# Recurrence inputs and gates of a hybrid block: activations stationary, tokens on partitions, blocks of 512 columns turned by transposes

## Chip, cores and metric

The kernel runs on one core of one Trainium2 chip. The metric is the device time of one execution in microseconds (us), as the median of several runs. The engines are called PE (TensorE, the matmuls), DVE (VectorE), ACT (ScalarE) and SP (SyncE, which issues the DMAs here). GpSimd takes next to no part in this kernel.

## What is computed

One block of a network for 256 tokens of width 2048, in fp32: a normalisation with a modulation from a second input, a mixer with two branches (sparse attention with three key sets, and a gated linear recurrence), and a gated feed-forward part with a short convolution. The change touches the two projections that feed the recurrence, `lx` and `ly`:

```python
def rg_lru(x, w_a, b_a, w_i, b_i, lam):
    xb = x.reshape(bn, t, LRU_BLOCKS, LRU_BLOCK_DIM)
    r = sigmoid(einsum('btnd,nde->btne', xb, w_a).reshape(bn, t, w) + b_a)
    i = sigmoid(einsum('btnd,nde->btne', xb, w_i).reshape(bn, t, w) + b_i)
    log_a = (LRU_C * r) * log_sigmoid(lam)
    a = exp(log_a)
    b = sqrt(-expm1(2.0 * log_a)) * (i * x)
    ...                     # h[t] = a[t] * h[t-1] + b[t]
    return h

def token_mixer(h, w_in, ...):
    z = h @ w_in
    q, kc, vc, ks, vs, kw, vw, g_nsa, lx, ly, ga, gb = split(z, ...)
    o_a = nsa_attention(q, kc, vc, ks, vs, kw, vw, g_nsa, ...)
    u = causal_dwconv(lx, conv_w, conv_b)
    o_b = gelu(ly) * rg_lru(u, w_a, b_a, w_i, b_i, lam)
    merged = sigmoid(ga) * (o_a @ proj_a) + sigmoid(gb) * (o_b @ proj_b)
    return merged @ w_out
```

Both `lx` and `ly` are 256 tokens by 2048 features, each a product of the normalised input (256 by 2048) with 2048 columns of `w_in`.

## The kernel before

All weights stream from HBM once. `stage` (line 97) loads a piece of 128x2048 into one of four buffers `raw`, and `split` (line 102) makes two rounded parts of each half of it: `hi` on ACT and `lo`, the rest, on DVE (lines 107 and 108), three buffers of each. A dense product is then three matmuls per tile of weights, `hi` with the high part of the input, `hi` with its low part, and `lo` with its high part. The input `h1` has both parts side by side, 256 columns each, with features on partitions.

Two forms of dense product concern us. `dense_pair1` (line 171) holds the weights stationary, 128x128 at a time, and moves the 256 tokens through: the result has features on partitions and tokens in columns, which is what the convolution along time and the scan of the recurrence need. Two tiles of 128 features share one accumulator bank of 512 columns, so a call makes 256 features in one bank, with 96 matmuls of 256 columns (lines 184, 186, 187). `dense_tok` (line 191) holds the activations stationary, 128 tokens at a time, and moves 512 columns of weights: the result has tokens on partitions, 128 tokens by 512 features in each of two banks, with 96 matmuls of 512 columns (lines 202 to 204). The merge, the output projection and the down projection use it already; where they need features on partitions again, they turn 128x128 tiles with transposes on PE (lines 760 and 803).

The accumulators come from `bank` (line 111), four banks in rotation. The other four PSUM banks have tags: "s" (two banks), "t" and "o" (one each). Attention uses them for scores (s), transposed probabilities (t) and its output (o), and the recurrence for its gate matmuls (s, t and o).

The order of work around the change, as the program is written, is: four blocks of queries with one attention unit (`attention`, line 589, one of 8) behind each; then the first loop (line 668), eight calls of `dense_pair1` that make `lx`, copied to SBUF by ACT (line 670), each followed by an attention unit while there are any and by two fillers (`filler`, line 477: a piece of the modulation vector, one DMA and one DVE row product); then the second loop (line 679), four rounds of the recurrence on 512 features each. A round has the convolution on DVE (lines 694, 697), the gate matmuls (lines 699, 701), sigmoid, tanh, exp and sqrt on ACT (lines 705 to 711, each change of function kind loads a table), products and the scan on DVE (lines 712 to 716), then two calls of `dense_pair1` for `ly`, each followed by Gelu on ACT (line 721), the product with the scan on DVE (line 722), and a split of it into `oB` (lines 725, 726). Behind this the merge begins (line 735).

A planner reorders instructions of each engine ahead of time by priorities and a model of the chip; on the chip each engine takes its own row of instructions in that fixed order and waits for semaphores. Slots of SBUF are shared by tag: `lx` has the tags C4 to C7, and C7 is also the slot of `cmpb`, which holds the compressed keys and values (`kcmp`, `vcmp`) that each attention unit reads (lines 597, 647). The tiles `u`, `r`, `iu`, `tt` of the rounds have the slots of `qT`, `kT` and `vN` of attention.

## Time and profile before

| | us |
|---|---|
| median of 3 runs | 1811.32 (1810.37 to 1814.28) |
| profiled execution | 1810.84 |
| its span | 1809.0 |
| PE busy | 1788.1 |
| DVE busy | 1338.8 |
| ACT busy | 867.3 |

The span is the time from the first to the last instruction of the program in the profile; the device time has 1.8 us more around it. The busy time of an engine is the time in which at least one of its instructions ran. On PE, weight loads and matmuls overlap, and a matmul begins before the one ahead has left the array, so its duration in a row is longer than the step to the next start. A wait is the idle time of an engine ahead of an instruction, put down to what released it last. PE ran at a granted clock of 1.00 for all but the first microseconds.

### The profile page before, as it was taken

The page shows a single profiled execution, that of the slowest core. Times are in us where ns is not written, and L with a number is a line of the kernel's source. Part 1 is how long each engine was busy: PE and PEld are TensorE (multiplying, and loading weights), DVE is VectorE, ACT ScalarE, POOL GpSimd, SP SyncE. Part 2 cuts the span into 40 slices and gives each one's busy share as a digit, 9 for nine tenths or more (in the row PEclk, how much of TensorE's full clock was granted, in tenths as well). Part 3 has the DMA queues.
Part 4 walks back from the last instruction along what each step waited for, and adds up shares of the span by engine and source line. Part 5 has one row for each costly group of instructions (what it writes and reads, how often), then busy time and mean ns, then how long its engine had stood idle before and what let it go on. Part 6 is the DMA issues. An engine that isn't in the chain of part 4 may idle for free.

```text
span 1809.0 us, 25836 instructions
## 1 busy us (share of the span) xinstructions
PE 1788.1 (99%) x10344; PEld 1555.3 (86%) x10344; DVE 1338.8 (74%) x1942; ACT 867.3 (48%) x1176; POOL 0.2 (0%) x4
## 2 busy tenths in 40 slices
PE   8999999999999999999999999999999999999998
PEld 7899898788899888888888998888888888888886
DVE  7999866898788866767666898888555666666555
ACT  5645434655578443434445544444433444444443
POOL 0000000000000000000000000000000000000000
PEclk9999999999999999999999999999999999999999
DMA  9999862666556768787776566777655555555553
GB/s 357 366 333 361 316 245 96 214 227 210 210 175 222 273 241 292 282 285 284 294 278 209 172 231 235 277 279 279 249 190 189 188 189 189 191 190 190 186 189 113
DMA packets 64201, 429.51 MB, mean 237 GB/s; under 512 B 7089, under 2 KB 7377, under 8 KB 15569
## 3 DMA queue, kind: packets, MB, share of 16 engines
q1 hardware_dynamic: 63792, 427.08, 66.3%
q8 instruction: 81, 1.33, 0.3%
q10 hardware_dynamic: 288, 0.79, 0.1%
q14 instruction: 40, 0.32, 0.1%
HBM read 425.72 MB, written 2.11 MB: 237 GB/s over the span
## 4 chain that ended last, share of the span: by engine, by line
PE 94%; DVE 3%; DMA 1%; ACT 1%; issue 1%; DVEq 0%; ACTq 0%
PE P L130 17%; PE P L203 11%; PE P L204 11%; PE P L202 11%; PE P L131 9%; PE P L187 3%; PE P L184 3%; PE P L186 3%; PE P L426 2%; PE P L428 2%; PE P L427 2%; PE P L420 2%; PE P L421 2%; PE P L419 1%; PE P L148 1%; PE P L147 1%
## 5 line engine op out<-in xcount | busy, mean ns | idle before, releaser
L107 ACT ACTIVATE hi<-raw 128x1024 fp32r<-128x1024 f32 x589 | 623.2, 1060 | 808.9 <-PE P L204 322.0
L108 DVE TENSOR_TENSOR lo<-raw,hi 128x1024 fp32r<-128x1024 f32 x589 | 718.6, 1223 | 388.1 <-ACT hi L107 387.1
L130 PE MATMUL P<-h,hi 128*128 128x512 f32 x1344 | 465.9, 397 | 0.0
L131 PE MATMUL P<-h,lo 128*128 128x256 f32 x1344 | 362.8, 280 | 0.0
L130 PEld LDWEIGHTS P<-h,hi 128*128 128x128 f32 x1344 | 246.7, 188 | 53.2
L131 PEld LDWEIGHTS P<-h,lo 128*128 128x128 f32 x1344 | 253.6, 189 | 7.7
L233 DVE SCALAR_TENSOR_TENSOR raw<-raw,crow 128x2048 f32<-128x2048 f32 x64 | 146.3, 2286 | 13.0 <-DMA raw<-ada_w 13.0
L187 PE MATMUL P<-h,lo 128*128 128x256 f32 x512 | 147.1, 288 | 2.1 <-DVE lo L108 2.1
L184 PE MATMUL P<-h,hi 128*128 128x256 f32 x512 | 146.7, 287 | 0.0
L186 PE MATMUL P<-h,hi 128*128 128x256 f32 x512 | 146.6, 286 | 0.0
L426 PE MATMUL P<-h,hi 128*128 128x256 f32 x384 | 108.0, 286 | 0.0
L427 PE MATMUL P<-h,hi 128*128 128x256 f32 x384 | 107.3, 284 | 0.0
L428 PE MATMUL P<-h,lo 128*128 128x256 f32 x384 | 102.2, 284 | 0.0
L187 PEld LDWEIGHTS P<-h,lo 128*128 128x128 f32 x512 | 97.7, 191 | 3.9 <-DVE lo L108 2.6
L184 PEld LDWEIGHTS P<-h,hi 128*128 128x128 f32 x512 | 97.9, 191 | 3.3 <-issue 3.0
L186 PEld LDWEIGHTS P<-h,hi 128*128 128x128 f32 x512 | 97.9, 191 | 1.1 <-issue 1.0
L203 PE MATMUL P<-lo,ua 128*128 128x512 f32 x240 | 93.4, 389 | 0.0
L204 PE MATMUL P<-hi,ua 128*128 128x512 f32 x240 | 93.4, 389 | 0.0
L202 PE MATMUL P<-hi,ua 128*128 128x512 f32 x240 | 83.6, 389 | 0.0
L203 PE MATMUL P<-lo,h 128*128 128x512 f32 x192 | 75.5, 393 | 0.6 <-DVE lo L108 0.5
L204 PE MATMUL P<-hi,h 128*128 128x512 f32 x192 | 74.9, 390 | 0.0
L426 PEld LDWEIGHTS P<-h,hi 128*128 128x128 f32 x384 | 74.1, 193 | 0.2
(265 smaller groups left out, 3121.9 us busy)
## 6 DMA issues: line engine op xcount, KB each, us to landing
raw<-ada_w SPq DMA_DIRECT2D x96, 1024.0 KB, 5.0
raw<-w_up SPq DMA_DIRECT2D x96, 1024.0 KB, 4.9
raw<-w_down SPq DMA_DIRECT2D x48, 1024.0 KB, 4.9
raw<-w_lru SPq DMA_DIRECT2D x32, 1024.0 KB, 5.0
raw<-w_proj SPq DMA_DIRECT2D x32, 1024.0 KB, 5.0
raw<-w_gates SPq DMA_DIRECT2D x24, 1024.0 KB, 6.4
raw<-w_out SPq DMA_DIRECT2D x16, 1024.0 KB, 5.0
raw<-w_kv SPq DMA_DIRECT2D x24, 512.0 KB, 6.8
```

The costliest lines, as they stand in the source:

```text
L107: A.activation(hi[:, :n], raw[:, lo_col:lo_col + n], AF.Copy)
L108: V.tensor_tensor(lo[:, :n], raw[:, lo_col:lo_col + n], hi[:, :n].bitcast(F32), op=ALU.subtract)
L130: PE.matmul(ps[f], hi[:, sl], r, start=(kt == 0), stop=False, skip_group_check=True)
L131: PE.matmul(o, lo[:, sl], r[:, 0:256], start=False, stop=(kt == n - 1), skip_group_check=True)
L184: PE.matmul(o, hi[:, sl], r[:, 0:256], start=(kt == 0 and f == 0), stop=False, skip_group_check=True)
L186: PE.matmul(o, hi[:, sl], r[:, 256:512], start=False, stop=False, skip_group_check=True)
L187: PE.matmul(o, lo[:, sl], r[:, 0:256], start=False, stop=(kt == n - 1), skip_group_check=True)
L202: PE.matmul(ps[j], xh, hi[:, w], start=(kt == 0), stop=False, skip_group_check=True)
L203: PE.matmul(ps[j], xh, lo[:, w], start=False, stop=False, skip_group_check=True)
L204: PE.matmul(ps[j], xl, hi[:, w], start=False, stop=(kt == n - 1), skip_group_check=True)
L233: V.scalar_tensor_tensor(raw, raw, 1.0, row, op0=ALU.mult, op1=ALU.mult, accum_out=modc[:, c:c + 1])
L426: PE.matmul(o, hi[:, sl], h1[:, kt, 0:256], start=first and f % 2 == 0, stop=False, skip_group_check=True)
```

## The change

Both loops use `dense_tok` instead of `dense_pair1`, 512 features at a time, with the weights packed for it. A new helper, `turned`, makes eight transposes of 128x128 on PE that turn a block back, into two banks of the same rotation of four. In the first loop ACT copies the two banks of the product to SBUF (into the place where the turned block goes later), and then the two turned banks over them. In the second loop the Gelu takes the place of the first copy, and the DVE product reads the turned banks from PSUM. The first loop now has four rounds with two attention units and four fillers each; the fillers of the second loop stand behind a round. `dense_pair1` goes; `dense_pair` loses an option that nobody used.

```diff
+        def turned(rows):
+            ps = [bank("turn"), bank("turn")]
+            for f in range(4):
+                for j in range(2):
+                    o = (f % 2) * 256 + j * 128
+                    PE.transpose(ps[f // 2][:, o:o + 128], rows[:, j, f * 128:f * 128 + 128], ident)
+            return [p.rearrange("p (f t) -> p f t", f=2) for p in ps]
...
-        for pr in range(8):
-            pl = dense_pair1([w_lru[pr, k] for k in range(2)], h1r)
-            A.activation(lx[pr // 2][:, 2 * (pr % 2):2 * (pr % 2) + 2],
-                         pl.rearrange("p (f t) -> p f t", f=2), AF.Copy)
-            if units:
-                attention(*units.pop(0))
-            filler(2)
+        for bt in range(4):
+            ps = dense_tok([w_lru[bt, k] for k in range(4)], h1r)
+            rows = lx[bt].rearrange("p (j a) t -> p j (a t)", j=2)
+            for j in range(2):
+                A.activation(rows[:, j], ps[j], AF.Copy)
+            for h, p in enumerate(turned(rows)):
+                A.activation(lx[bt][:, 2 * h:2 * h + 2], p, AF.Copy)
+            for _ in range(2):
+                if units:
+                    attention(*units.pop(0))
+            filler(4)
...
-            for h in range(2):
+            ps = dense_tok([w_lru[4 + bt, k] for k in range(4)], h1r)
+            rows = u.rearrange("p (j a) t -> p j (a t)", j=2)
+            for j in range(2):
+                tbl(A.activation(rows[:, j], ps[j], AF.Gelu_apprx_tanh))
+            for h, p in enumerate(turned(rows)):
                 pr = bt * 2 + h
-                pl = dense_pair1([w_lru[8 + pr, k] for k in range(2)], h1r)
                 gl = u[:, 2 * h:2 * h + 2]
-                tbl(A.activation(gl, pl.rearrange("p (f t) -> p f t", f=2), AF.Gelu_apprx_tanh))
-                V.tensor_tensor(gl, gl, iu[:, 2 * h:2 * h + 2], op=ALU.mult)
+                V.tensor_tensor(gl, p, iu[:, 2 * h:2 * h + 2], op=ALU.mult)
...
-                filler(2 if pr % 4 == 0 else 0)
+            filler(2 if bt % 2 == 0 else 0)
...
-    a["w_lru"] = np.concatenate([_pack(w[:, 5168:7216]), _pack(w[:, 7216:9264])])
+    a["w_lru"] = _tok(w[:, 5168:9264])
```

The planner's order changes with it. Numbers behind a name tell buffers of one name apart; a row of the changed kernel has that kernel's own line numbers (L178 to L180 are the three matmuls of `dense_tok` there, L207 the transposes, L658 and L660 the copies of the first loop, L689 and L691 the gate matmuls, L710 the Gelu).

PE near the end of the first loop, before: the fourth head of the last attention unit but its tail (`tp`, transposed probabilities), its product with the compressed values (`oT_4438<-pcT_4461,cmpb_204`), and dense matmuls of the seventh and the eighth call (`P_4820`, `P_4946`).

```order
L643 MATMUL tp_4502<-cols_113,p_4491 128x128 x4
L647 MATMUL oT_4438<-pcT_4461,cmpb_204 128x512
L184 MATMUL P_4820<-h1_169,hi_4909 128x256
L186 MATMUL P_4820<-h1_169,hi_4909 128x256
L184 MATMUL P_4946<-h1_169,hi_4949 128x256
L186 MATMUL P_4946<-h1_169,hi_4949 128x256
L187 MATMUL P_4820<-h1_169,lo_4910 128x256
L184 MATMUL P_4820<-h1_169,hi_4909 128x256
```

The same place of the changed kernel, the last two attention units (`oT_4155`, `oT_4262`), the first gate matmuls of the recurrence (`lru_r`), and the first dense matmul of the second loop (`P_4793`) behind two transposes of the first loop's last block (`turn`).

```order
L629 MATMUL tp_4253<-cols_113,p_4242 128x128 x2
L689 MATMUL lru_r_4742<-lt_4736,raw_4740 128x256 x2
L637 MATMUL oT_4155<-pT_4180,vN_203 128x512 x2
L599 MATMUL tpc_4280<-cols_113,pc_4268 15x128 x4
L629 MATMUL tp_4304<-cols_113,p_4293 128x128 x4
L629 MATMUL tp_4326<-cols_113,p_4315 128x128 x4
L633 MATMUL oT_4262<-pcT_4285,cmpb_204 128x512
L689 MATMUL lru_r_4756<-lt_4736,raw_4740 128x256 x2
L207 MATMUL turn_4708<-cols_113,lx_3529 128x128
L207 MATMUL turn_4709<-cols_113,lx_3529 128x128
L178 MATMUL P_4793<-hi_4797,h1_169 128x512
```

Before, dense matmuls of two different banks stand around the last unit's product with `cmpb`. Now attention's rows follow each other from the first loop's last dense matmul to the transposes, and the second loop's first dense matmul stands behind these.

PE where one call for `ly` ends and the next one begins, before: the first two calls of the second loop (`P_5129`, `P_5259`).

```order
L184 MATMUL P_5129<-h1_169,hi_5218 128x256
L186 MATMUL P_5129<-h1_169,hi_5218 128x256
L187 MATMUL P_5129<-h1_169,lo_5219 128x256
L184 MATMUL P_5259<-h1_169,hi_5262 128x256
L186 MATMUL P_5259<-h1_169,hi_5262 128x256
```

The changed kernel: the end of the second loop's first block (`P_4794`, its second half of the tokens), gate matmuls of the next round, the first two transposes of the block (`turn`, from `lt_4736`, into which the Gelu writes), and the next block (`P_5014`).

```order
L179 MATMUL P_4794<-lo_4916,h1_169 128x512
L180 MATMUL P_4794<-hi_4915,h1_169 128x512
L689 MATMUL lru_r_4963<-lt_4959,raw_4961 128x256
L691 MATMUL lru_i_4964<-lt_4959,raw_4961 128x256
L689 MATMUL lru_r_4963<-lt_4959,raw_4961 128x256
L691 MATMUL lru_i_4964<-lt_4959,raw_4961 128x256
L689 MATMUL lru_r_4977<-lt_4959,raw_4961 128x256 x2
L691 MATMUL lru_i_4978<-lt_4959,raw_4961 128x256 x2
L207 MATMUL turn_4933<-cols_113,lt_4736 128x128
L207 MATMUL turn_4934<-cols_113,lt_4736 128x128
L178 MATMUL P_5014<-hi_5018,h1_169 128x512
```

Before, the next call follows in another bank with nothing between. Now the transposes of a block, which read what the Gelu wrote, stand ahead of the next block.

ACT ahead of the first Gelu of the second loop (L721 before), before: the chain of sigmoid, tanh, exp, sqrt with its table loads, and splits (L107) for later weights.

```order
L706 ACTIVATE lt_5074<-lru_i_5093,cols_113 128x256
L107 ACTIVATE hi_5218<-raw_5188 128x1024
L709 ACTIVATE lt_5075<-lt_5073 128x512
L107 ACTIVATE hi_5262<-raw_5260 128x1024
L710 ACT_TABLE_LOAD
L710 ACTIVATE lt_5073<-lt_5073 128x1024
L711 ACT_TABLE_LOAD
L711 ACTIVATE lt_5075<-lt_5075 128x1024
L107 ACTIVATE hi_5290<-raw_5260 128x1024
L107 ACTIVATE hi_5320<-raw_5318 128x1024
L721 ACT_TABLE_LOAD
L721 ACTIVATE lt_5072<-P_5129 128x512
```

The changed kernel, where the Gelu has L710 and reads the block `P_4793`, `P_4794`:

```order
L695 ACTIVATE lt_4737<-lru_r_4756,cols_113 128x256
L696 ACTIVATE lt_4738<-lru_i_4757,cols_113 128x256
L699 ACTIVATE lt_4739<-lt_4737 128x512
L700 ACT_TABLE_LOAD
L700 ACTIVATE lt_4737<-lt_4737 128x1024
L701 ACT_TABLE_LOAD
L701 ACTIVATE lt_4739<-lt_4739 128x1024
L107 ACTIVATE hi_5052<-raw_5050 128x1024
L710 ACT_TABLE_LOAD
L710 ACTIVATE lt_4736<-P_4793 128x512
L710 ACTIVATE lt_4736<-P_4794 128x512
```

The chain is the same; three of the splits that stood inside it are elsewhere now, and the last gate that it reads, `lru_i_4757`, comes from a matmul near the end of the same block.

## Rows read from the trace of the kernel before

**Rows 1.** The page: busy us (share) xinstructions; the last chain by engine.

```profile
PE 1788.1 (99%) x10344; PEld 1555.3 (86%) x10344; DVE 1338.8 (74%) x1942; ACT 867.3 (48%) x1176; POOL 0.2 (0%) x4
...
PE 94%; DVE 3%; DMA 1%; ACT 1%; issue 1%; DVEq 0%; ACTq 0%
```

**Rows 2.** Windows of the two loops: length, busy us (instructions) by engine, PE clock, DMA.

```profile
333.00:490.00 157.00, 157.00 (x1080) 130.63 (x1079) 130.07 (x336) 82.61 (x203) 0.00 (x0) 1.00 0.59 209
490.00:598.00 108.00, 105.94 (x831) 103.61 (x830) 92.35 (x131) 85.19 (x112) 0.00 (x0) 1.00 0.58 207
```

**Rows 3.** Waits of PE at 320 to 620 us: total, times, longest.

```profile
PE P L187 <- DVE lo L108: 2.1, 2, 1.5
```

**Rows 4.** Timeline of PE in the second loop, 256 columns: start, us, instruction.

```profile
559.92 0.28 PE L184 MATMUL P<-h,hi 128*128 128x256 f32 x1
...
561.96 0.28 PE L187 MATMUL P<-h,lo 128*128 128x256 f32 x1
```

**Rows 5.** Timeline of PE in the merge, dense_tok with 512 columns.

```profile
619.76 0.39 PE L202 MATMUL P<-hi,oB 128*128 128x512 f32 x1
...
625.88 0.39 PE L203 MATMUL P<-lo,oB 128*128 128x512 f32 x1
```

**Rows 6.** Timeline of PE: four transposes between dense matmuls of the merge.

```profile
921.46 0.39 PE L204 MATMUL P<-hi,mg 128*128 128x512 f32 x1
921.69 0.60 PE L760 MATMUL turn<-cols,sg 128*128 128x128 f32 x4
...
922.36 0.40 PE L204 MATMUL P<-hi,mg 128*128 128x512 f32 x1
```

**Rows 7.** Timeline of ACT: first chain of the second loop, with splits (L107).

```profile
494.66 0.46 ACT L706 ACTIVATE lt<-lru_i,cols 128x256 f32<-128x256 f32 x1
...
495.73 1.07 ACT L107 ACTIVATE hi<-raw 128x1024 fp32r<-128x1024 f32 x1
...
497.50 1.06 ACT L107 ACTIVATE hi<-raw 128x1024 fp32r<-128x1024 f32 x1 [0.18 <-ACT lt L709]
498.59 1.28 ACT L710 ACT_TABLE_LOAD   x1
...
504.50 1.06 ACT L107 ACTIVATE hi<-raw 128x1024 fp32r<-128x1024 f32 x1 [0.26 <-PE P L186]
...
506.88 0.60 ACT L721 ACTIVATE lt<-P 128x512 f32<-128x512 f32 x1
```

**Rows 8.** Timeline of PE: attention at 438 to 462 us; two rows a matmul.

```profile
441.77 1.02 PE L621 MATMUL s<-kT,qT 128*128 128x512 f32 x2
...
442.74 1.08 PE L621 MATMUL s<-kT,qT 128*128 128x512 f32 x2
...
445.69 1.12 PE L647 MATMUL oT<-pcT,cmpb 15*128 15x512 f32 x2
...
458.98 1.88 PE L651 MATMUL oT<-pT,vN 128*128 128x512 f32 x4
```

**Rows 9.** Chain of work in order of time: start, us, what (one gate matmul).

```profile
500.66 0.43 PE lru_r L699 x2
```

**Rows 10.** Timeline of ACT: attention at 438 to 462 us.

```profile
442.02 0.57 ACT L615 ACTIVATE pcT<-tpc 15x512 f32<-15x512 f32 x1
445.67 0.38 ACT L645 ACTIVATE pT<-tp 128x256 f32<-128x256 f32 x1 [3.08 <-PE tp L643]
446.90 0.48 ACT L633 ACTIVATE p<-s,sm 128x256 f32<-128x256 f32 x1 [0.85 <-DVE sm L631]
...
447.37 0.47 ACT L633 ACTIVATE p<-s,sm 128x256 f32<-128x256 f32 x1
```

**Rows 11.** Timeline of DVE, same stretch: a maximum over scores.

```profile
446.72 0.68 DVE L630 TENSOR_REDUCE sm<-s 128x2 f32<-128x512 f32 x1
```

**Rows 12.** Window near the start of the kernel.

```profile
19.80:23.00 3.20, 3.19 (x15) 3.20 (x16) 3.20 (x4) 0.90 (x1) 0.00 (x0) 0.51 0.96 373
```

**Rows 13.** Timeline of PE there; in brackets its wait and who ended it.

```profile
19.81 1.22 PE L426 MATMUL hold<-h,hi 128*128 128x256 f32 x4 [2.23 <-ACT h L291]
```

27 lines of the change are left out of this document (2 added, 25 removed).

## The prediction

> **What bounds the kernel now.** I read the page's shares first: TensorE (PE) is busy for 99% of the span, and the chain that ended last runs through it for 94% [rows 1]. So the time is what PE issues plus what it waits. The two loops that the change touches lie at 333 to 598 us [rows 2]. There PE is full, VectorE (DVE) has 83% and 86%, ScalarE (ACT) 53% and 79%. The view of waits shows 2.1 us of PE waiting in this stretch [rows 3]: work on the other engines costs nothing here until it makes PE wait. PE is pipelined, so the price of a matmul is not the duration in its row but the distance between two starts. The change leaves the bytes, the splits and the recurrence as they are, and the order of the instructions differs only between the last attention units and the end of the second loop.
>
> **Fewer, longer matmuls.** Before, a block of 512 features takes 4 x 16 x 3 = 192 matmuls of 256 columns. Seventeen steps from 559.92 to 561.96 are 2.04 us, 0.1200 us each [rows 4]. After, it takes 2 x 16 x 3 = 96 of 512 columns; twenty-seven steps from 619.76 to 625.88 are 6.12 us, 0.2267 us each [rows 5]. Two short ones cost 0.2400, one long one 0.2267: 13.3 ns go with each matmul saved. For 8 blocks that is 1536 x 0.1200 = 184.3 against 768 x 0.2267 = 174.1: **-10.2 us**, all of it on PE's path. Bounds: 0, if a long one takes as much as two short ones in these loops, and -10.2, the rows.
>
> A rule speaks against this size. The Trainium skill (TensorE: Matmul & The Clock Gate, section Back-to-back issue gap) gives a fixed cost of about 2.5 ns per matmul at the full clock; an estimate by that page is 768 x 2.5 ns = 1.9 us of gain instead of 10.2. The rows here show five times that, and I take the rows.
>
> **The transposes.** New on PE are 8 blocks x 8 = 64 transposes of 128x128. The kernel has the same instruction further down, four of them between two dense matmuls. From 921.46 to 922.36 pass 0.90 us where two dense steps would be 0.45, so four cost 0.45 and each further one 0.11 [rows 6]. The order puts them as 2 and 6 into each block: about 0.24 + 0.67 = 0.91, times 8 is **+7.3 us**. So the arithmetic alone gives -2.9 us, and waits of a few us decide the sign.
>
> **What ACT and DVE get.** The first loop gains 8 evictions of 128x512 on ACT, 0.60 us each [rows 7]: 4.8 us that lie in ACT's idle 74 us of that loop [rows 2]. In the second loop the Gelu count stays 8, and DVE's product reads PSUM instead of SBUF. These cost nothing as long as PE doesn't wait for them. It does once per block: the first two transposes stand right behind the block and need the eviction of its first half. Over these 0.60 us lie the six matmuls of the second half (1.36 us), unless ACT is inside a split of 1.06 us [rows 7]. Bounds: 0 and 8 x 1.06 = 8.5 us; I take a value near 0, since the cover is twice the eviction: **+0.9 us**.
>
> **Banks, the new wait.** Four accumulator banks rotate. Before, a block of 256 features takes one, so PE can be four blocks (46 us) ahead of ACT. After, a block of 512 takes two and its transposes two: the next block's accumulators are the two just filled, and PE can start on them only behind the evictions. Two evictions are late.
>
> *Place A, end of the first loop.* lx[3] has the slot of cmpb, which the last attention unit reads until its matmul with vcmp. Before, one bank waits for that and PE goes on in the next. After, both banks wait, and the order has a stretch of attention without a dense matmul ahead of the transposes. Its PE work from the first score matmul: four scores at 0.97, two value products at 0.86, two with pcT at 1.05 [rows 8], four gate matmuls at 0.43 [rows 9] and 20 transposes at 0.11 [rows 6], together 11.7 us. The chain through the softmax is longer. In it two exps take 1.0 us, a copy of a turned tile 0.3, oA and pcT some 0.55 each [rows 10], a maximum 0.6 to 0.7 [rows 11], a table load 1.28 [rows 7]. Walking down PE's, ACT's and DVE's rows with these, from that score matmul: the exps of head 0 end at 3.7, of head 1 at 5.0 (the third and fourth scores wait for their bank), of head 2 at 7.2 (the gate matmul waits for its bank), table and sigmoid at 9.2, oA and pcT (behind the value products) at 11.0, the next copies at 12.4, table and exps of head 3 at 14.7, two copies at 15.3, the block's eviction at 15.8. PE's transposes come at 15.9, not 11.7: **+4.3 us** of waits in some eight pieces. Bounds: 0 if other work covers them, 7 if DVE's conv rows, which stand among the softmax rows, hold it up.
>
> *Place B, end of the second loop's first block.* As attention ends inside this block, the recurrence's first chain starts late in it. The last three sigmoids follow a gate matmul that has only 10 dense (2.3 us) and 8 gate matmuls (3.4 us, [rows 9]) behind it; then come the transposes, which need the Gelu. Before, from the first of the three sigmoids at 494.66 to the Gelu's end at 507.48 passed 12.8 us, with three splits of together 3.1 in them that now stand elsewhere [rows 7]: 9.7, and some 0.4 from PE to ACT and back. The Gelu ends 10.1 us behind that matmul, against 5.7 of work: **+4.4 us** in one piece, bounds 0 and 6. Before, it came with PE already in the next bank. In the later blocks the chain starts at the block's beginning and lies under 22.7 us of PE work.
>
> **The sum.** The profiled execution took 1810.84 us (span 1809.0 and 1.8 around it), 0.5 under the median 1811.32. 1810.8 - 10.2 + 7.3 + 0.9 + 4.3 + 4.4 = **1817.5 us**. The 2.1 us of old waits are left in: they came from splits late on DVE, whose load stays. 0.2% of the time before is 3.6 us (about what a measurement can tell from no change), so "same" is 1807.7 to 1814.9.
>
> **Rivals.**
> 1. *Only one of the two waits is there.* If attention ends earlier against the dense work than I read from the order, B goes, or A's pieces are covered: 1817.5 - 4.4 = 1813.1, no change. For it: both are sums of short pieces, and PE may come to these rows late enough that the softmax is done. Against: A's waits follow from PSUM tags one deep inside the stretch, whoever comes first.
> 2. *Faster: the banks don't bind.* Every eviction comes in time, because ACT and DVE stay ahead of PE as they are now; it decides from waits under about 1 us in all. Then -2.9 + 0.9, and the old 2.1 us gone as well: 1806 to 1809, middle 1807. For it: ACT has nearly half its time free in the first loop [rows 2]. Against: ACT takes its rows in order, and the order itself has the stretch without dense work.
> 3. *The clock falls.* After a wait of 2.23 us that ended at 19.8 us, PE ran at a granted clock of 0.51 (1.2 of 2.4 GHz) for 3.2 us [rows 12, 13], which loses half of these, 1.6 us. If B, or B and A, sets that off: 1819.1 to 1820.7. The same page of the Trainium skill (section Why this matters for your kernels) warns of idle gaps between bursts of matmuls for this reason; the rows at 19.8 us agree.
> 4. *The cost per matmul is not saved.* If a long matmul took as much as two short ones here, the first term is 0: 1810.8 + 7.3 + 0.9 + 8.7 = 1827.7. The spacings speak against it [rows 4, 5]. By the 2.5 ns of the page above it would be 1825.8.
>
> That the change doesn't do what it says is out: the order shows the 768 and the 64 instructions.
>
> **Chances.** Forecast 0.50; one wait only 0.25; faster 0.13; clock 0.07; no saving per matmul 0.05. Slower by over 0.2% is 0.50 + 0.07 + 0.05 = 0.62, within it 0.25, faster 0.13. The forecast's own range is 1814.9 to 1822. For 8 in 10 the range goes down into the faster case and up past the clock case and A's upper bound: 1807 to 1824. Left out are the lower half of the faster case, the case without saving and the tail.
>
> **What the profile after would show.** Dense starts 0.227 us apart and transposes 0.11: the terms -10.2 and +7.3. PE's waits in this stretch: a sum near 9 to 12 us, the longest one ahead of the first transposes of the second loop, released by the Gelu (B), and several under 1 us among the last attention rows, released by exps, copies and the first loop's last eviction (A). Behind the second loop nothing differs. I am wrong in B if the Gelu of that block ends before PE's last gate matmul, in A if PE has no gap over 0.2 us among the last attention rows, and in the arithmetic if the spacings differ.

## The result

The changed kernel takes 1828.66 us (median of 4 runs, 1826.01 to 1829.28), the kernel before 1811.60 in the same comparison: a ratio of 1.0087, 95% interval 1.0075 to 1.0100. It is slower, as forecast, but by 17 us and not by 6.7, and the time lies above the range. The profiled execution took 1829.13 us with a span of 1827.3.

The page of the changed kernel, busy times and the last chain (to compare with [rows 1]):

```profile
PE 1797.0 (98%) x9640; PEld 1524.0 (83%) x9640; DVE 1341.7 (73%) x1942; ACT 878.4 (48%) x1188; POOL 0.2 (0%) x4
...
PE 92%; DVE 3%; ACT 2%; DMA 1%; issue 1%; DVEq 0%; ACTq 0%
```

PE has 704 instructions less (1536 dense ones before; 768 dense ones and 64 transposes after), and yet is busy for 9 us more. Part of the reason is the clock: at half clock the same instruction keeps PE busy longer. Windows of the changed kernel between 477 and 551 us (length, busy us and instructions of PE, weight loads, DVE, ACT and POOL, then the granted clock, the DMA share, GB/s):

```profile
477.00:490.00 13.00, 10.60 (x40) 5.79 (x39) 11.15 (x38) 9.31 (x23) 0.00 (x0) 0.85 0.00 1
486.00:492.90 6.90, 6.90 (x16) 4.29 (x16) 2.43 (x11) 2.97 (x9) 0.00 (x0) 0.51 0.00 0
527.00:530.40 3.40, 2.99 (x8) 2.47 (x9) 1.38 (x2) 3.37 (x7) 0.00 (x0) 0.50 0.01 2
547.50:550.90 3.40, 3.40 (x10) 2.66 (x9) 3.40 (x6) 1.06 (x1) 0.00 (x0) 0.50 0.69 280
```

The last three run at half clock (1.2 of 2.4 GHz); in both loops of the kernel before it was 1.00 [rows 2]. The first is place A: forty matmuls in 13 us, hardly a transfer. The view of waits for PE at 333 to 614 us, the two loops of the changed kernel (to compare with [rows 3]: what waited, for what, total, times, longest):

```profile
PE P L179 <- DVE lo L108: 5.1, 5, 1.9
PE turn L207 <- ACT lt L710: 3.9, 1, 3.9
PE lru_r L689 <- ACT p L619: 0.9, 1, 0.9
PE tp L629 <- ACT pT L631: 0.7, 1, 0.7
PE tp L629 <- ACT pcT L601: 0.7, 1, 0.7
PE P L178 <- ACT hi L107: 0.2, 1, 0.2
```

The second row is place B, in one piece, released by the Gelu (L710). The next three are place A. The first row was not in the forecast: late splits, 2.1 us before, are 5.1 now.

**Where 18 us went.** I took every step from one start on PE to the next, between the transposes of the gate tile (`gtp`, at 288 us, ahead of both loops) and those of `mq` (in the merge, 647 us before, 664 after). A step's usual length for its kind is *work*; in a stretch at half clock, up to the same length again is *clock*; the rest is *waits*. This is arithmetic on the trace's rows, the same for each kernel; which length is taken as usual moves up to about 1 us from one column to another, mostly between clock and waits, and leaves the sum as it is. The stretch is 17.9 us longer: work -3.2, clock +6.2, waits +14.9. Of the waits 10.6 us lie in steps stretched by over 0.25 us (A 2.9, B 4.0, and late splits some 4 more than before); the other 4.3 us are many short ones, which the view of waits doesn't name. Behind the stretch another 0.4 us come.

**The path.** The attention's last product starts 195.2 us behind the gate tile in the kernel before, 221.9 us in the changed one; from there to the first matmul of the merge's projections it is 114.2 us before, 104.2 now. So attention ends 26.6 us later; about 10 us of this are made good in the second loop, and 16.7 reach the projections. Why it ends later is seen in the turns of one attention unit's four heads. Timeline of PE, the transposes `tp`, before:

```profile
445.26 0.38 PE L643 MATMUL tp<-cols,p 128*128 128x128 f32 x2
...
449.00 0.38 PE L643 MATMUL tp<-cols,p 128*128 128x128 f32 x2
...
452.50 0.38 PE L643 MATMUL tp<-cols,p 128*128 128x128 f32 x2
...
455.89 0.38 PE L643 MATMUL tp<-cols,p 128*128 128x128 f32 x2
```

The same in the changed kernel:

```profile
448.53 0.60 PE L629 MATMUL tp<-cols,p 128*128 128x128 f32 x4
...
454.34 0.60 PE L629 MATMUL tp<-cols,p 128*128 128x128 f32 x4
...
459.94 0.60 PE L629 MATMUL tp<-cols,p 128*128 128x128 f32 x4
...
464.65 0.60 PE L629 MATMUL tp<-cols,p 128*128 128x128 f32 x4
```

A head takes 3.5 us before and 5.4 us now. Between two such steps the instruction order has some 20 dense matmuls in both kernels: 2.4 us of 256 columns, 4.5 us of 512. The planner has put as many between as before, each nearly twice as long. So the order differs from the first loop's start on, and not only from the last attention units on.

### The profile page after: what moved, and what is told of

It reads as the page before. It is cut to its first block, busy times and chain, and to the rows that moved or that the text cites. A ratio compares the mean times of both kernels' runs of the same rounds, so it can differ in the third digit from the quotient of the medians.

```text
span 1827.3 us, 24410 instructions
## 1 busy us (share of the span) xinstructions
PE 1797.0 (98%) x9640; PEld 1524.0 (83%) x9640; DVE 1341.7 (73%) x1942; ACT 878.4 (48%) x1188; POOL 0.2 (0%) x4
## 4 chain that ended last, share of the span: by engine, by line
PE 92%; DVE 3%; ACT 2%; DMA 1%; issue 1%; DVEq 0%; ACTq 0%
PE P L126 17%; PE P L179 14%; PE P L180 14%; PE P L178 14%; PE P L127 9%; PE P L412 2%; PE P L413 2%; PE P L414 2%; PE P L406 2%; PE P L407 2%; PE P L405 1%; PE P L144 1%; PE P L143 1%; PE P L145 1%; PE oT L637 1%; PE s L607 1%
## 5 line engine op out<-in xcount | busy, mean ns | idle before, releaser
L107 ACT ACTIVATE hi<-raw 128x1024 fp32r<-128x1024 f32 x589 | 622.6, 1060 | 814.3 <-PE P L180 360.0
L127 PE MATMUL P<-h,lo 128*128 128x256 f32 x1344 | 362.8, 280 | 0.0
L126 PEld LDWEIGHTS P<-h,hi 128*128 128x128 f32 x1344 | 246.8, 188 | 53.2
L127 PEld LDWEIGHTS P<-h,lo 128*128 128x128 f32 x1344 | 253.6, 189 | 7.7
L179 PE MATMUL P<-lo,h 128*128 128x512 f32 x448 | 180.1, 402 | 5.7 <-DVE lo L108 5.7
L180 PE MATMUL P<-hi,h 128*128 128x512 f32 x448 | 177.5, 396 | 0.0
L178 PE MATMUL P<-hi,h 128*128 128x512 f32 x448 | 166.9, 400 | 0.6 <-ACT hi L107 0.6
L219 DVE SCALAR_TENSOR_TENSOR raw<-raw,crow 128x2048 f32<-128x2048 f32 x64 | 146.3, 2286 | 11.3 <-DMA raw<-ada_w 11.2
L412 PE MATMUL P<-h,hi 128*128 128x256 f32 x384 | 108.2, 286 | 0.0
L179 PEld LDWEIGHTS P<-lo,h 128*128 128x128 f32 x448 | 85.2, 190 | 27.2 <-DVE lo L108 9.3
L413 PE MATMUL P<-h,hi 128*128 128x256 f32 x384 | 107.6, 284 | 0.0
L414 PE MATMUL P<-h,lo 128*128 128x256 f32 x384 | 102.1, 284 | 0.0
L178 PEld LDWEIGHTS P<-hi,h 128*128 128x128 f32 x448 | 85.1, 191 | 18.7 <-ACT hi L107 1.6
L180 PEld LDWEIGHTS P<-hi,h 128*128 128x128 f32 x448 | 85.1, 190 | 18.4 <-issue 1.5
L180 PE MATMUL P<-hi,ua 128*128 128x512 f32 x240 | 93.4, 389 | 0.0
L178 PE MATMUL P<-hi,ua 128*128 128x512 f32 x240 | 83.6, 389 | 0.0
L412 PEld LDWEIGHTS P<-h,hi 128*128 128x128 f32 x384 | 74.1, 193 | 0.2
L413 PEld LDWEIGHTS P<-h,hi 128*128 128x128 f32 x384 | 74.2, 193 | 0.0
L308 DVE SCALAR_TENSOR_TENSOR raw<-raw,crow 128x2048 f32<-128x2048 f32 x31 | 70.8, 2285 | 2.4 <-DMA raw<-ada_w 2.1
```

Source lines behind the costliest of these rows:

```text
L107: A.activation(hi[:, :n], raw[:, lo_col:lo_col + n], AF.Copy)
L126: PE.matmul(ps[f], hi[:, sl], r, start=(kt == 0), stop=False, skip_group_check=True)
L127: PE.matmul(o, lo[:, sl], r[:, 0:256], start=False, stop=(kt == n - 1), skip_group_check=True)
L178: PE.matmul(ps[j], xh, hi[:, w], start=(kt == 0), stop=False, skip_group_check=True)
L179: PE.matmul(ps[j], xh, lo[:, w], start=False, stop=False, skip_group_check=True)
L180: PE.matmul(ps[j], xl, hi[:, w], start=False, stop=(kt == n - 1), skip_group_check=True)
```

## Experiments

All times are compared with runs of the kernel before on the same chip (median 1810.9 to 1812.0 in the five comparisons). The table has the ratio with its interval (from all runs), and from the one profiled execution the sums as defined above (against before, us) and the path: the start of the attention's last product behind the gate tile, and from there to the first projection matmul.

| kernel | ratio (95%) | work | clock | waits | attention ends | then |
|---|---|---|---|---|---|---|
| before | 1 | 0 | 0 | 0 | 195.2 | 114.2 |
| after | 1.0087 (1.0075–1.0100) | -3.2 | 6.2 | 14.9 | 221.9 | 104.2 |
| e1 first loop only | 1.0113 (1.0095–1.0131) | -1.7 | 8.7 | 13.9 | 223.5 | 104.2 |
| e2 second loop only | 1.0034 (1.0021–1.0047) | -1.7 | 0 | 7.9 | 195.9 | 118.0 |
| e3 slot freed | 1.0110 (1.0095–1.0126) | -3.2 | 6.7 | 17.5 | 229.5 | 99.7 |
| e4 copy first | 1.0071 (1.0057–1.0085) | -3.2 | 0 | 16.0 | 219.4 | 98.7 |
| e5 halves | 1.0090 (1.0076–1.0104) | 6.9 | 0 | 8.0 | 196.1 | 127.0 |
| e6 paced | 1.0070 (1.0058–1.0083) | -3.2 | 4.6 | 12.3 | 214.5 | 107.3 |
| e7 filled wait | 1.0134 (1.0118–1.0149) | 0.9 | 7.1 | 15.9 | 221.9 | 109.2 |
| e9 before, no tables | 0.9990 (0.9980–1.0000) | -0.2 | 0 | -1.7 | 195.4 | 112.2 |
| e10 second loop, no tables | 1.0035 (1.0022–1.0047) | -1.7 | 1.6 | 5.1 | 195.2 | 118.0 |
| e11 after, no tables | 1.0037 (1.0023–1.0050) | -3.2 | 0 | 8.8 | 219.0 | 94.7 |
| e12 second loop, not turned | 1.0028 (1.0016–1.0040) | -5.1 | 3.1 | 7.8 | 195.7 | 119.4 |
| e13 second loop, turned pairs | 1.0140 (1.0126–1.0154) | 3.3 | 4.1 | 17.0 | 195.3 | 138.5 |
| e17 second loop, spread | 1.0037 (1.0024–1.0050) | -1.7 | 0 | 9.5 | 195.2 | 118.3 |
| e18 spread, copy first | 1.0051 (1.0039–1.0064) | -1.7 | 3.2 | 8.8 | 195.8 | 121.4 |

The profiled execution also differs by up to 3.4 us ahead of the gate tile, where no kernel was changed; the sums and the path leave this out, the ratios do not.

### One loop at a time

e1 has `dense_tok` and `turned` in the first loop alone, e2 in the second alone.

> The first loop as after, the second loop as before. Theory (place A costs waits and also a clock drop, and both belong to the first loop): half of the arithmetic, about -1 us, place A's waits +4, one stretch of 6.8 us at 1.2 GHz +3.3, and no wait for a Gelu ahead of transposes: about +6, 1818 us (1816 to 1820), granted clock 0.5 once, near the end of the attention. Rival 1 (nearly all of the loss is made in the second loop): 1811 to 1813 us. Rival 2 (attention that ends late harms the second loop whatever its form): 1821 us or more, with several us of waits behind the attention.

> The second loop as after, the first loop as before. Theory (the second loop has its own wait at its first block, the recurrence's chain being longer than the PE work behind the gate matmuls): -1 us of arithmetic, 2 to 3 us of wait ahead of the first transposes, later split waits of some 2 to 3 us more than before, one clock drop of 1.7 us at most: 1815 us (1813 to 1818). Rival 1 (the second loop only inherits the late attention of the first): no wait over 1 us there, no drop of the clock, 1809 to 1811 us. Rival 2 (the second loop makes nearly all of the loss by itself): 1822 us or more.

The first loop alone costs as much as the whole change, if not more: 1832.55 us (the intervals meet). It has attention 28 us late. At the end of attention, at 480 to 504 us, lie 17.0 of its 20.4 us at half clock, and then a second loop of the old form pays as well, with a wait of 5.0 us for a late split:

```profile
PE P L180 <- ACT hi L107: 5.3, 2, 5.0
```

That is rival 2 of e1, and my theory fell. The second loop alone took 1817.72 us, some 6 us over before (ratio 1.0034), with the clock at 1.00 in both loops; its waits at 333 to 640 us:

```profile
PE P L199 <- DVE lo L108: 4.9, 6, 1.6
PE turn L227 <- ACT lt L726: 0.9, 3, 0.3
```

So place B needs the late attention (three waits of at most 0.3 us here), and the second loop has a loss of its own, most of it late splits (4.9 of 7.9 us of waits). The time of e2 lies in my range, but not for my reason: the wait of 2 to 3 us ahead of the first transposes, on which the range was built, isn't there.

### Place A: the slot, or the order

e3 moves `kcmp` and `vcmp` out of C7. e5 cuts each dense matmul of the loops in two and leaves all else. e6 frees the slot, keeps 512 columns, writes all attention units ahead of the first loop and ties that loop's dense matmuls behind the attention's steps.

```diff
-        kcmp = cmpb[:, 256:316]
-        vcmp = cmpb[0:16, 316:828]
+        kcmp = small["gap5"][:, 0:60]
...
+            c3.append(big.tile([128, 1024], F32, tag="C3", name="c3"))   # e3: vcmp in its upper half
```

```diff
+                    for c in range(cut):                                  # e5: cut=2 in the two loops
+                        z = 512 // cut
+                        w, o = slice(k * 512 + c * z, k * 512 + c * z + z), ps[j][:, c * z:c * z + z]
```

```diff
+                    if pace and k == 0:                                   # e6, order only
+                        i = calls[0] * 36 // 64 - 3
...
+                            tc.add_manual_dep(m.ins, marks[i].ins.name, NOSYNC, reason="pace")
```

> The kernel after, with the compressed keys and values moved out of slot C7 (keys into a spare column range, values into the unused half of slot C3), so that lx[3] has its slot to itself. Theory (place A is the shared slot with both banks blocked): the stretch of attention without dense work goes from the end of the first loop, with it its waits of about 4 us and the stretch at 1.2 GHz behind them (3.3 us); the wait ahead of the first transposes of the second loop stays or grows by 1 to 2 us: about 1822 us (1820 to 1824). Rival 1 (the clock falls for another reason than the waits): the drop near 486 us stays and the time is 1825 us or more. Rival 2 (the attention's own chain sets the end, and the wait only moves behind the next block): 1827 to 1830 us, no change.

> The kernel after, but each dense matmul of the two loops cut into two of 256 columns; layout, transposes and bank use as after. The instruction order of this kernel has the attention steps between the dense matmuls as the kernel before has them (some 20 dense matmuls between two steps, which take 2.4 us here and 4.5 us with 512 columns), and no stretch of attention without dense work. Theory (what is lost is the order: as many dense matmuls stand between two steps of the attention as before, each twice as long, so attention ends some 27 us late and is left bare): dense work back to its 184 us, 64 transposes at +7 us, the waits of place A and the clock drops gone: about 1818 us (1816 to 1821), faster than after although TensorE has 10 us more of dense work. Rival 1 (banks and transposes make the waits): all waits and drops stay and the dense work adds its 10 us: 1837 us. Rival 2 (only place A belongs to the order, the second loop's waits belong to the banks): 1824 us.

> The kernel after with 512 columns kept, the slot C7 freed for lx[3], and the dense matmuls of the first loop tied in groups of six to the steps of the attention units by order alone (no semaphore), so that about half as many stand between two steps. Theory (the order makes the loss): attention ends near 490 us instead of 509 us, no bare stretch at its end, no clock drop in the loops beyond one at most; what is left is the second loop's waits as in the kernel with the second loop alone: 1811 to 1816 us. Rival 1 (512 columns, banks and turning cost it whatever the order): 1824 us or more. Rival 2 (the second loop's waits follow from the late attention too): 1809 us or less.

e3 took 1831.73 us. The stretch of bare attention went from the first loop's end, but came back behind the next block: at 509 to 514 us three steps of 0.89 to 1.32 us stand among attention's rows (the third row below has two of them), with 6.8 us at half clock from 512 us on, and a longer wait came at place B. Its view of waits, 333 to 640 us:

```profile
PE turn L207 <- ACT lt L711: 6.0, 2, 5.6
PE P L179 <- DVE lo L108: 3.9, 4, 1.8
PE tp L630 <- ACT pT L632: 1.8, 2, 1.1
```

Attention ended even later (229.5), so the slot and the banks only decided where TensorE waits for it: rival 2, whose range (1827 to 1830) the time lies a little above.

e5 has the same layout, transposes and banks as after and 10 us more work, and is not slower than after (1827.30). Attention ends at 196.1 us again, the place A waits are gone, and the clock stays at 1.00 in the loops. Its heads, timeline of PE:

```profile
449.83 0.38 PE L632 MATMUL tp<-cols,p 128*128 128x128 f32 x2
...
453.28 0.38 PE L632 MATMUL tp<-cols,p 128*128 128x128 f32 x2
...
456.78 0.38 PE L632 MATMUL tp<-cols,p 128*128 128x128 f32 x2
```

3.5 us a head, as before: the length of the matmuls between the steps, whose number stays, makes attention late, not layout, banks or slot. But the time is 9 us above my 1818, and above rival 2's 1824: 8.0 us of waits stay, 4.6 of them late splits in the view of waits. So the second loop's waits don't go with attention's late end, as e2 (waits 7.9) says too. e6 points the same way with 512 columns: fewer matmuls between the steps bring attention's end back by 7.4 us against after, and by 15.0 against e3, which frees the slot too. Its time of 1824.51 is not what I hoped for (1811 to 1816) and lies where rival 1 has it: a bare stretch of attention moved to the start of the loop (350 us, 3.4 us at half clock), and a wait of 3.6 us for `hi` came in the second loop, with 6.8 us at half clock behind it. It brought back 7.4 of 26.6 us only, so it doesn't decide between theory and rival 1; e5 does, for attention.

### Place B: the Gelu on TensorE's path

e4 copies a block out of its banks at once, turns it, and takes the Gelu of the turned block; this adds two copies of 128x512 per round on ACT. e7 puts 18 matmuls ahead of the first transposes of the second loop, in the place of the wait.

```diff
+            with tc.high_priority(200):                                   # e4
+                for j in range(2):
+                    A.activation(rows[j], ps[j], AF.Copy)
...
+                tbl(A.activation(gl, p, AF.Gelu_apprx_tanh))
```

```diff
+            for n in range(extra):                                        # e7: extra=18 in the first round
+                m = PE.matmul(ps[0], h1r(n % KT)[:, 0:128], h1r(n % KT), start=True, stop=True, skip_group_check=True)
+                tc.add_manual_dep(m.ins, behind.ins.name, NOSYNC, reason="behind the gates")
```

> The kernel after, with the second loop's blocks copied out of their banks at once (a Copy ahead of the queued rows, into two spare tiles), turned, and the Gelu taken of the turned block. Theory (place B is the transposes waiting for a Gelu at the end of the recurrence's chain): the wait of 3.9 us ahead of the first transposes goes, and the clock drop behind it (1.7 us); the later split waits of 6 to 7 us, which follow from the chain being bunched behind that wait, shrink: 1820 us (1818 to 1823). Rival (the split waits come from the load on ACT and DVE in this loop, which the wait at B only spaced out): B goes but the split waits grow by as much, 1825 to 1829 us.

> The kernel after with 18 matmuls of 512 columns more (4.1 us), whose results are overwritten by the transposes: they stand on TensorE ahead of the first transposes of the second loop, where the kernel after waits 3.9 us for the Gelu. Theory (the clock falls behind a wait): the wait is filled, the drop to 1.2 GHz at 527 us does not come, and the time is 1.7 us lower than after, or the same if nothing else moves: 1826 to 1829 us, with the drop at 486 us still there. Rival (the drop has nothing to do with the wait): drops at 527 us as before, and the time is 4 us longer wherever the filling is longer than the wait: 1830 to 1833 us.

e4 took 1824.79 us. The wait for the Gelu is gone and the clock doesn't fall in the loops, but the splits are later than in after (9.1 us against 5.1). Its waits, 333 to 640 us:

```profile
PE P L179 <- DVE lo L108: 9.1, 9, 1.7
```

That is the rival's mechanism, and the time lies between the two ranges; the eight copies more on ACT may have their share in the late splits, which no run tells apart. What the profiled execution gained against after is the clock (6.2 us), not the waits (16.0 against 14.9). Half of this gain can't be put down to the edit: 6.8 of after's 13.6 us at half clock come at place A, and e4 has the same steps there without a drop. In e7 the drop at 527 us did not come, since the wait there was filled; a wait of 4.3 us for `hi` then came at 537 us, with a drop behind it, and the time rose to 1835.56, above both ranges. The waits stayed as they were in sum (15.9 against 14.9), and the 4.1 us of filling came on top:

```profile
PE P L178 <- ACT hi L107: 5.5, 2, 4.3
PE P L179 <- DVE lo L108: 4.4, 5, 1.5
```

### The second loop's late splits

The splits are late in rows like these, ACT and then DVE of the changed kernel ahead of a wait of 1.90 us that ended at 545.98:

```profile
537.63 1.28 ACT L700 ACT_TABLE_LOAD   x1
538.92 1.06 ACT L700 ACTIVATE lt<-lt 128x1024 f32<-128x1024 f32 x1
539.99 1.28 ACT L701 ACT_TABLE_LOAD   x1
541.28 1.06 ACT L701 ACTIVATE lt<-lt 128x1024 f32<-128x1024 f32 x1
542.25 2.93 ACT L107 ACTIVATE hi<-raw 128x1024 fp32r<-128x1024 f32 x3
```

```profile
542.38 1.23 DVE L703 SCALAR_TENSOR_TENSOR lt<-lt 128x1024 f32<-128x1024 f32 x1 [1.68 <-ACT lt L701]
543.52 1.26 DVE L687 SCALAR_TENSOR_TENSOR lt<-lx,cols,lt 128x253 f32<-128x253 f32 x3
544.70 1.22 DVE L108 TENSOR_TENSOR lo<-raw,hi 128x1024 fp32r<-128x1024 f32 x1
```

Exp and square root with their table loads stand ahead of three splits on ACT, and the conv ahead of `lo` on DVE. I took the suspects away one by one. e8 leaves the four modulation pieces out of the second loop (done later); e9 (on before), e10 (on e2) and e11 (on after) take all its table functions as Copy (the recurrence's functions are left out); e12 is e2 without the transposes (the gate branch is not turned back); e13 turns blocks of 256 features, two per round; e14 (on e2), e15 (on before) and e16 (on after) have four buffers of split halves and three of staged weights; e17 ties four rows of the chain behind splits; e18 adds the early Copy to e17.

```diff
-            filler(2 if bt % 2 == 0 else 0)                               # e8
...
-            tbl(A.activation(tt, tt, AF.Sqrt))                            # e9 to e11, and so on
+            A.activation(tt, tt, AF.Copy, scale=0.01)
...
-            for h, p in enumerate(turned(rows)):                          # e12
+            for h, p in enumerate([u[:, 0:2], u[:, 2:4]]):
...
+                pl = dense_tok1([w_lru[8 + pr, k] for k in range(2)], h1r)     # e13: one bank, 256 columns
...
-                into = [wpool.tile([128, 1024], F32R, tag=t_, bufs=3, name=t_) for t_ in ("hi", "lo")]
+                into = [wpool.tile([128, 1024], F32R, tag=t_, bufs=4, name=t_) for t_ in ("hi", "lo")]   # e14 to e16
...
+            tbl(behind(A.activation(tt, tt, AF.Sqrt), 5))                 # e17, e18: behind the 6th split
```

> The kernel with only the second loop changed, without the four modulation pieces (2.3 us of VectorE each) that this loop takes in; they are done in later stages. Theory (the split waits of the second loop come from the order of VectorE's rows, the lo half standing behind longer rows there): two of the six waits of about 5 us in all go, 1815 to 1816 us. Rival 1 (VectorE's load as such is the limit of this loop): 9 us less of load take the waits away, 1811 to 1812 us. Rival 2 (the pieces have nothing to do with it): 1817 to 1819 us.

> Control. The kernel before, with all the table functions of the second loop (sigmoid, tanh, exp, square root, Gelu) taken as Copy: the recurrence's values are left out, the instructions and their sizes stay, and ACT loads no table there (1.28 us each, up to five per round). Theory (the waits for late splits come from ACT's chain of table functions): the 2 to 3 us of split waits of before go, 1808 to 1810 us. Rival (VectorE's load makes them): no change, 1811 us.

> The kernel with only the second loop changed, and its table functions taken as Copy as in the control (the recurrence's values are left out). Theory (with one block per round both Gelus stand together and the next round's chain follows at once, so that ACT has a run of 11 to 12 us with few splits in it, longer than the stock of three split halves; without the table loads the run is 5 us shorter): the waits of some 8 us fall to 2 us or less, and the kernel comes to within 1 us of the control or under it: 1808 to 1811 us. Rival (banks and transposes, or VectorE's rows, make the waits): 4 to 6 us over the control, 1813 to 1817 us.

> The kernel after, with the table functions of the second loop taken as Copy (the recurrence's values are left out). Theory: the second loop's waits go, place B and the clock drops behind it among them; place A's waits of 4 us stay, with or without the drop behind them (3.3 us): 1812 to 1817 us. Rival (banks and transposes make the second loop's waits): 1822 us or more.

> The kernel with only the second loop changed, and its 32 transposes left out (the gate branch goes on with tokens on partitions, so its values are wrong; all else stays). Theory (ACT's chain makes the split waits): 3.5 us of transposes and the 0.9 us of waits ahead of them go, the split waits of 5 us stay: 1812 to 1814 us. Rival (the transposes and their two banks hold TensorE up and with it the splits): all of it goes, 1808 us or less.

> The kernel before with the second loop alone turned to tokens on partitions, but in blocks of 256 features, two per round: 96 matmuls of 256 columns, one Gelu and four transposes each, in one bank and one bank more for the turned block. Theory (one block of 512 features per round bunches the second loop's rows: both Gelus, both products and the next round's chain follow one another, and the splits come late behind them): the dense work is that of before, 32 transposes add 3.5 us, the waits stay at the 2 to 3 us of before and the clock does not fall: 1814 to 1816 us. Rival (it is the turning itself, with transposes that need the Gelu, that makes TensorE wait): waits of 6 us or more, 1818 us or more.

> The kernel with only the second loop changed, with four buffers for the split halves instead of three, and three for the staged weights instead of four, in the whole kernel. Theory (TensorE outlasts a late split by its stock of split halves, 2.7 us each): one half more takes 2.7 us from each of the waits, of some 8 us in all 2 us or less stay, and no clock drop: 1809 to 1812 us, within 1 us of its control. Rival 1 (VectorE's rows as a whole are the limit there, so a longer stock only moves the wait): 1816 us or more. Rival 2 (three staging buffers are too few for the transfers): its control is slower than before too.

> Control: the kernel before with four buffers for the split halves and three for the staged weights. Theory: the 2 to 3 us of waits for late splits go, 1808 to 1810 us. Rival (three staging buffers are too few): waits for transfers all over the kernel, 1815 us or more.

> The kernel after with four buffers for the split halves and three for the staged weights. Theory: the waits for late splits go; place A (waits some 4 us, and 3.3 us of lower clock in some runs) and place B (4 us, and 1.7) stay: 1819 to 1823 us. Rival 1 (the stock changes nothing): 1826 us or more. Rival 2 (the waits at A and B also go): 1812 us or less.

> The kernel with only the second loop changed; in each round the block's splits are now written ahead of the recurrence's chain, and four rows of the chain on ACT are tied by order alone behind the 2nd, 4th, 5th and 6th split, so that sigmoids and splits stand mixed as in the kernel before (first Gelu to square root in a row: four to six splits between instead of three or four). Theory (late splits come from the order of ACT's rows, the chain standing in one piece ahead of a bunch of splits): the waits of some 8 us fall to 4 us or less, 1811 to 1814 us. Rival (the limit is the round's own chain, from the conv to the Gelu, that TensorE now meets at its transposes): split waits are exchanged for waits ahead of the transposes, 1816 us or more.

> The kernel of e17 with the blocks copied out of their banks ahead of the chain and the Gelu taken of the turned block, so that no row of TensorE needs the chain before the next block's transposes. Theory (order of ACT's rows): as e17 or up to 2 us less, 1809 to 1813 us, no wait over 1 us ahead of transposes. Rival (the chain and the splits together are more than ACT and VectorE can serve in order within a round of 26 us): waits of 6 us or more remain as split waits, 1816 us or more.

**Table loads** (e9 to e11). In the kernel before they cost little: 1809.70 us without them, against 1811.29, in my range, with an interval that just reaches no change. The changed kernel without them is 10.7 us faster: e11 took 1817.94, just above my range, and the stretch behind attention is 94.7 instead of 104.2 us. Not all of this is the loads' own time: by the table 6.2 us are the clock, which doesn't fall in e11, not at place A either, ahead of the second loop; the waits are 6.1 us less. Place B is gone from the view of waits, but 4.0 of 5.1 us of late splits stay. That fits the path above (where attention ends late, the recurrence's rounds on ACT and DVE hold TensorE up), but is argued, not shown. With attention on time the loads cost nothing that can be told: e10 took 1817.65 and e2 1817.72, and e10 is 8 us over its control e9, more than the rival's 4 to 6; late splits are 4.2 us. My theory fell there.

**Turning against grouping** (e12, e13). Blocks in the old pairs, but turned, are the worst form of the second loop: e13 took 1836.70 us, since TensorE now meets nearly each pair's Gelu (the rival). Its waits, 333 to 640 us:

```profile
PE turn L744 <- ACT lt L740: 15.2, 7, 4.3
PE P L206 <- DVE lo L108: 1.7, 2, 1.0
```

The late splits are down to 1.7 us here, near the 2.1 of before, but that doesn't show that grouping makes them: in the 15.2 us that TensorE waits for a Gelu, splits can catch up. In e12 (1816.14 us, above both ranges), blocks of 512 without transposes, they stay and are longer:

```profile
PE P L199 <- DVE lo L108: 7.4, 4, 4.1
```

So in the pairs TensorE waits at the transposes and in the blocks at the splits; neither part of the change is free by itself, and with both (e2, waits 7.9) the waits are no more than with the blocks alone (7.8).

**The other suspects.** e8's late splits stayed (5.6 us in the view of waits), and its stretch up to `mq` is 6.7 us over before, against 6.2 in e2; its time, 1829.14 (ratio 1.0099, 1.0085 to 1.0113), tells nothing of this loop, since 9.5 us of it were lost later, between `mq` and the output projection, with 10.2 us at half clock at 916 us; no expectation had that. A longer stock could not be had cheaply: with three staging buffers the kernel before takes 1857.20 us (e15), waiting up to 12.5 us for `hi` far behind the loops, e14 1864.36 and e16 1872.28 (the rival of too few staging buffers); in the second loop, e14 still had 4.2 us of late splits and 3.2 us ahead of transposes. But in e16 the late splits are less than half of after's 5.1 us (view of waits, 333 to 660 us), while place B stays (4.2 us):

```profile
PE P L179 <- DVE lo L108: 2.2, 3, 1.3
```

By the same arithmetic as in the table its stretch up to `mq` is 11.9 us over before, against 17.9 in after. So a longer stock may well help with the late splits; what it costs in staging hides this in the time. Mixing ACT's rows gave 1819.24 (e17), with the early Copy 1822.43 (e18); late splits 6.1 and 7.4 us. So neither the four pieces nor the mix of rows, as far as these edits change it, is the cause; my theory for e17 and e18 was wrong, and the rivals' times fit. No version beat the kernel before clear of noise; e9, which leaves the recurrence's functions out, is at 0.9990 (0.9980 to 1.0000).

What makes the splits late in blocks of 512 is not settled. Transposes (e12), table loads (e10) or modulation pieces (e8) alone don't make them, and e17's mix of ACT's rows doesn't cure them. That one `dense_tok` block per round leaves ACT and DVE with the whole round's rows at once, in an order that none of these edits got right, is argued, not shown. A kernel with a longer stock of split halves and all four staging buffers would tell more, and was not tried.

## Why the prediction was right and wrong

- **Arithmetic, -10.2 and +7.3**: right. Work is -3.2 against -2.9. Dense steps in the changed loops have a median of 0.227 us (0.2267 in [rows 5]), transposes 0.109 (0.11 in [rows 6]). Two short matmuls less one long one are 13 ns. The 2.5 ns of the Trainium skill (TensorE: Matmul & The Clock Gate, section Back-to-back issue gap) are not what these rows show.
- **Place B, +4.4**: right in mechanism and size, 3.9 us in one piece, released by the Gelu, and there only where attention ends late (e2). Timeline of PE there:

```profile
522.49 1.03 PE L691 MATMUL lru_i<-lt,raw 128*128 128x256 f32 x4
527.41 0.69 PE L207 MATMUL turn<-cols,lt 128*128 128x128 f32 x2 [3.90 <-ACT lt L710]
527.75 0.78 PE L178 MATMUL P<-hi,h 128*128 128x512 f32 x1
```

- **Place A, +4.3**: right in place, too large (three steps of 1.21, 0.99 and 1.02 us at 478 to 485 us, 2.9 us over their usual length; the view has 2.3), and wrong in its reason. I put it on the shared slot with both banks blocked. e3 freed the slot, and the waits came back one block later; e5 took them away with slot and banks as they are. The reason is the order: attention ends 26.6 us late. The step behind it is "the order of the instructions differs only between the last attention units and the end of the second loop": already the first unit of the first loop has heads of 5.4 to 6.7 us, against 3.9 to 4.3 before. (The sum of PE's work in that stretch is 11.6 by its own rows, not 11.7.)
- **The evictions, +0.9**: the view shows no wait of this kind, but for 0.2 us for `hi`, which is a split.
- **The waits' sum, 9 to 12 us**: the view shows 11.5, or 9.4 more than before, against 9.6 forecast. That is luck: A, B and the evictions came out 3.4 us smaller, and late splits, forecast at no change, 3.0 us larger. Steps give 14.9. The failed step is "The 2.1 us of old waits are left in: they came from splits late on DVE, whose load stays", together with the chain that in the later blocks "lies under 22.7 us of PE work". No later transposes waited much, but the splits did: 5.1 us in five waits. DVE's load stayed (1341.7 us busy against 1338.8), and the splits were later all the same; why is open, as said above. This is the first mis-sized term, 5.3 us (14.9 against 9.6); late splits are some 4 us more than before by the steps, A, B and the evictions 2.7 less than forecast, and the rest, some 4 us, are the many short stretches, which the forecast had not and whose cause stays open.
- **The clock, 0 in the forecast**: the second term, 6.2 us. The mechanism was there as rival 3, at 0.07 and with 1.6 us per drop; three stretches, one of them twice as long, came together with A, B and a late split. What follows from the forecast's own waits should not have stood beside it as a rival with a small chance: 1817.5 + 6.2 + 5.3 gives 1829. At place A the drop is not a must: e4 has the same steps there and none, and the runs of after lie 3.3 us apart.
- **What is left with attention on time**: e2 and e5, both at full clock in the loops, still have some 8 us of waits. So attention's late end accounts for A, B and the stretches at half clock behind them, not for the whole.
- **"Behind the second loop nothing differs"**: nearly. 0.4 us come there, and 1.2 us of the last transposes lie among the projection's matmuls.

## What to carry to other kernels

Here the planner kept the number of matmuls between two steps of attention when each matmul got twice as long. So look in the new order for what now stands between the steps of a chain that waits for its own results, and price where that chain ends, not only the waits at the seams. An eviction with a table function that feeds a transpose puts the whole chain that ends in that function on TensorE's path (place B, e13); to take it off the path helps only if the splits don't come late instead (e4). And when a forecast holds waits of some us on TensorE, the lower clock behind them belongs in the same sum.

## What the runs showed of the hardware

- In the two loops of after, e1 to e13, e17 and e18, nine steps on PE (start to start) were 3.2 us or longer, and with each came 3.4 or 6.8 us at a granted clock of 0.5, the lower of the two levels (1.2 GHz), beginning in the step or just behind it. Of ten between 2.2 and 2.9 us that began at full clock, five were followed by one. A step of 2.07 us by itself (e4) was not. Rows of shorter ones went either way: steps of 1.54 and 1.19 us in e7 had a drop behind them; place A has steps of 1.21, 0.99 and 1.02 us in after, with a drop behind, and of 1.21, 0.99 and 1.02 us in e4, with none. The Trainium skill (TensorE: Matmul & The Clock Gate, section Why this matters for your kernels) warns of idle gaps between bursts of matmuls; the traces agree for the nine long ones.
- At the lower clock a 512-column step is 0.427 us instead of 0.227. Timeline of PE in the changed kernel, across the end of such a stretch:

```profile
529.61 0.63 PE L179 MATMUL P<-lo,h 128*128 128x512 f32 x1
530.03 0.57 PE L180 MATMUL P<-hi,h 128*128 128x512 f32 x1
530.44 0.40 PE L178 MATMUL P<-hi,h 128*128 128x512 f32 x1
530.68 0.39 PE L179 MATMUL P<-lo,h 128*128 128x512 f32 x1
```

- Three staging buffers of 1 MB instead of four, with four buffers of split halves instead of three, cost the kernel before 2.6% (e15, ratio 1.0256, 1.0236 to 1.0276).
